# Two more weight slots during the first attention of a fused two-block transformer kernel

## The chip, the cores and the metric

The kernel runs as one program on one core of a Trainium2 chip. The metric is the device time of one execution in microseconds (us); the median of three runs of the kernel before is 869.89 us, the lowest 868.91 and the highest 870.24. The profile that is read below is one execution of its own: it took 870.59 us, of which 868.7 us lie between its first and its last instruction (the span).

## The reference, cut to what matters

256 tokens of width 1024 in float32 go through two blocks. The first block is where the change lies:

```python
h = layer_norm(x, ln0_g, ln0_b)
proj = h @ w_in + b_in                    # split into qa, ka, va, qb, kb, vb, ga, gb
y_na  = neighbourhood_attention(qa, ka, va, rpb) @ w_branch_na
y_swa = windowed_gqa_with_sink(rope(qb), rope(kb), vb, sink) @ w_branch_swa
mixed = sigmoid(ga) * y_na + sigmoid(gb) * y_swa
h = layer_norm(ALPHA * h + mixed @ w_out + b_out, ln1_g, ln1_b)
h = layer_norm(ALPHA * h + relu(h @ w_ff1 + b)**2 @ w_ff2 + b, ln2_g, ln2_b)
```

The second block (a pooling mixer, a second attention, two convolutional feed-forward layers) follows and is computed by the same weight machinery.

## The kernel before, in words

All matrix products are kept near float32 accuracy by splitting both operands into a high part of type fp32r and a low part, the rest (`whi`, `wlo` for weights; `xh`, `xl` and the like for data), and by three matmuls per product: high by high, high by low, low by high (`mm3`, L367).

Weights come as a list of chunks of 128 x 1024 float32 (512 KB), numbered in the order in which the program uses them. The class `Weights` (L76) moves each chunk through three places. A raw buffer takes the DMA from memory (six such buffers for the first 48 chunks, then four); the load of chunk i + 6 is issued on the SP queue behind the split of chunk i. Splitting a chunk takes one instruction on ScalarE, the copy to `whi` (L133), and then one on VectorE, the subtraction that gives `wlo` (L143). The results lie in a slot (8 KB per partition) until the matmuls that use the chunk are done and `free` gives the slot back. There are seven slots, w0 to w6, in the pool `pers`; after the first attention two more and an extra one are added in the pool `late`, which takes over memory of the first attention.

The order of all instructions of every engine is the order of the Python program, and every engine runs its instructions in that order. So the splits have to be written somewhere, and this is done by `pump(most, eng, keep)`: it splits the next chunks, at most `most`, while more than `keep` slots are free. `unit_a` (L374) is the unit of work: it computes 256 output columns in two halves (m = 0 and 1) of 128. A half issues its matmuls into one PSUM bank, then calls the epilogue that empties the bank, then pumps: at most two chunks and keeping two slots (`KEEP`), or one in the units `bna`. With `ahead` the copy to `whi` is issued before the epilogue and the subtraction behind the epilogue's first part. The matmuls of a half go to one of four banks that are used in rotation (`bank`, tag "a").

The first attention uses chunks 0 to 41: qa and ka (0 to 7), va (8 to 11), qb and kb/vb (12 to 17), the gates ga (18 to 25), the branch `bna` (26 to 29: four units of one chunk, so eight halves of 12 matmuls each), the gates gb (30 to 37), and the last branch `swa` (38 to 41, again eight halves of 12 matmuls). The product with `w_out` uses chunks 42 to 49 (matmuls of 512 columns, `Acc`, L446).

A loop of ten steps (L752) carries the softmax work of eight head pairs: at step i the transposes of pair i - 2, the scores of pair i, the normalisation of pair i - 1, then units as fillers, then the product with the values of pair i - 2 (`pv1`). The fillers of step 6 are the four units of `bna`. Its epilogue (L644) is one VectorE instruction per half that reads the bank. The four `swa` units come after the loop; their epilogue (L784 to L791) is, per half, two VectorE instructions, one copy on ScalarE (`mixh`) and a third VectorE instruction (`mixl`).

The pools `att1o` and `att1` hold the first attention's data; both close behind `swa` (L799). In `att1` lie, among others, `row` (the first norm's gain, used once at the start), `va` (the values of the first four head pairs, last read by `pv1` of pair 3 in step 5), `mix` (two buffers) and ten buffers `fm`.

Of the kernel before, what the change touches and what calls it, by code (L numbers as in the profile page):

```python
# [5 lines left out]
F32 = mybir.dt.float32  # L6
# [6 lines left out]
P = 128  # L13
T = 256
D = 1024
# [3 lines left out]
LENT_FOR = 48  # L19
NW = 7  # L20
NW_LATE = 2
KEEP = 2
TAIL = 6
TAIL_FF = 8
# [51 lines left out]
class Weights:  # L76


    def __init__(self, nc, pool, wts, lent):
        self.lent, self.done = lent, 0  # L80
        self.nc, self.pool, self.wts, self.n = nc, pool, wts, wts.shape[0]
        self.raw, self.ready, self.slots, self.held = {}, {}, [], []
        self.loaded = self.split = self.taken = self.n_slots = 0
        self.before, self.gain, self.retired, self.todo, self.eager = {}, {}, set(), [], True
        self.at_split = set()
# [26 lines left out]
            self.before[i](self.raw[i])  # L112

    def pump(self, most=99, eng=None, keep=0):
        while most and len(self.slots) > keep and self.split < self.n:
            most -= 1
            self.high()(eng)

    def high(self):

        i = self.split
        while i in self.todo:
            self.prepare(1)
        r = self.raw.pop(i)
        slot = self.slots.pop(0)
        pool, tag = slot
        hi = pool.tile([P, 1024], F32R, tag=tag + "h", name="whi", bufs=1)
        lo = pool.tile([P, 1024], F32R, tag=tag + "l", name="wlo", bufs=1)
        for j, g in enumerate(self.gain.get(i, [])):
            d = slice(j * T, (j + 1) * T)  # L130
            self.nc.scalar.activation(out=hi[:, d], in_=r[:, d], func=AF.Identity, scale=g)
        if i not in self.gain:
            self.nc.scalar.activation(out=hi, in_=r, func=AF.Copy)  # L133
        self.ready[i] = (hi, lo, slot)
        self.split += 1

        def low(eng=None):
            for j, g in enumerate(self.gain.get(i, [])):
                d = slice(j * T, (j + 1) * T)
                self.nc.vector.scalar_tensor_tensor(out=lo[:, d], in0=r[:, d], scalar=g, in1=hi[:, d].bitcast(F32),  # L140
                                                    op0=ALU.mult, op1=ALU.subtract)
            if i not in self.gain:
                (eng or self.nc.vector).tensor_tensor(out=lo, in0=r, in1=hi.bitcast(F32), op=ALU.subtract)  # L143
            self.done += 1
            self.load()
        return low

    def highs(self, n):
        return [self.high() for _ in range(min(n, len(self.slots), self.n - self.split))]

    def take(self, k, c):

# [27 lines left out]
def model(tc, x_in, wts, bvec, cols_in, const_in, nab_in, pos_in, out):  # L180
    nc = tc.nc
    from contextlib import ExitStack
    with ExitStack() as top:
# [6 lines left out]
        def rot(pool, shape, dt, tag, name, bufs):  # L190

            key = (id(pool), tag)
            i = turn[key] = (turn.get(key, -1) + 1) % bufs
            return pool.tile(shape, dt, tag=f"{tag}_{i}", name=name, bufs=1)
# [4 lines left out]
        def pad(pool, n):  # L199

            pool.tile([P, 8 * n], F32, name=f"pad_{len(pads)}", tag=f"pad_{len(pads)}", bufs=1)
            pads.append(n)
# [6 lines left out]
        ctx_g, ctx_x = ExitStack(), ExitStack()  # L209
        gpool = ctx_g.enter_context(tc.tile_pool(name="gates", bufs=1))  # L210
        opool = ctx_x.enter_context(tc.tile_pool(name="att1o", bufs=1))
        apool = ctx_x.enter_context(tc.tile_pool(name="att1", bufs=1))

        pad(com, PAD_COM)
# [2 lines left out]
        def scratch():  # L217
            return rot(com, [P, D], F32, "scr", "scr", 4)

        def vec(row, eng=None, pool=None, tag="bv", bufs=4):  # L220
            v = rot((pool or com), [P, D], F32, tag, f"v{row}", bufs)
            (eng or nc.gpsimd).dma_start(out=v, in_=bvec[row:row + 1, :].broadcast_to([P, D]))
            return v

        for t in range(2):
            x_t.append(scratch())
        for s in HALF:
            nc.sync.dma_start(out=x_t[0][:, s], in_=x_in[0:P, s])
        row = apool.tile([1, D], F32, name="row")
        nc.scalar.dma_start(out=row, in_=bvec[V_G0:V_G0 + 1, :])  # L230
        b0 = vec(V_B0, nc.sync)
        W = Weights(nc, pers, wts, [(com, "scr_2"), (com, "scr_3")])
        W.grow(pers, NW)
        W.load(3)
        nc.sync.dma_start(out=x_t[1], in_=x_in[P:T, :])
        W.load(NRAW + 2 - 3)
# [137 lines left out]
        def unit_a(kx, epi, nk=8, pump=(2, None), ahead=0):  # L374

            cs = [W.take(4, 256) for _ in range(nk // 4)]
            for m in range(2):
# [9 lines left out]
                for low in lows:  # L387
                    low()
                W.pump(0 if ahead else pump[0], pump[1], keep=KEEP)
                for f in later:  # L390
# [55 lines left out]
        class Acc:  # L446
# [15 lines left out]
            def both(self, k, x):  # L462
# [3 lines left out]
                W.free(c)  # L466
                W.pump(2, keep=KEEP)

# [27 lines left out]
        lows = W.highs(2)  # L496
# [19 lines left out]
        def load_const(pool, name, at, n, shape=None):  # L516
            c = pool.tile([P, n], F32, name=name)
            nc.sync.dma_start(out=c, in_=const_in[:, at:at + n])
            const[name] = c
            return c  # L520
# [3 lines left out]
        def load_nab(p):  # L524
            nab[p] = rot(apool, [P, 2, 384], F32, "nab", "nab", 2)
            nc.sync.dma_start(out=nab[p], in_=nab_in[p])
# [4 lines left out]
        fm = {}  # L531
# [34 lines left out]
        nc.sync.dma_start(out=vab, in_=bvec[V_VAB:V_VAB + 1, 0:512].broadcast_to([P, 512]))  # L566


        va = apool.tile([P, 2, 512], F32, name="va")
        vb = apool.tile([P, 2, P], F32, name="vb")  # L570

        def f_va():
# [143 lines left out]
        def transp1(p):  # L716
            pt = soft[p][0]
            ptT[p] = []
            for e in range(2):
                b = bank("b")  # L720
                for s in range(2):
                    for j in range(2):
                        nc.tensor.transpose(out=b[:, s * T + j * P:s * T + (j + 1) * P],
                                            in_=pt[e][:, j, s * P:(s + 1) * P], identity=ident)
                c = rot(apool, [P, 512], F32, "pT", "pT", 2)
                nc.scalar.activation(out=c, in_=b, func=AF.Copy)
                ptT[p].append(c)
# [13 lines left out]
        def step(n=1):  # L741
            for _ in range(n):
                next(fill, None)
# [8 lines left out]
        for i in range(10):  # L752
            if i == 1:
                swam = load_const(apool, "swam", K_SWA, 512)
                sink = few.tile([P, 24], F32, name="sink")
                nc.sync.dma_start(out=sink, in_=bvec[V_SINK:V_SINK + 1, 0:24].broadcast_to([P, 24]))
                bout = vec(V_BOUT, nc.sync)
            if i == 6:
                g1 = vec(V_G1, nc.sync)
                b1 = vec(V_B1, nc.sync)  # L760
            if i >= 2:
                transp1(i - 2)
            if i < 8:
                scores1(i)
                if i + 2 < 4:
                    load_nab(i + 2)
            if 1 <= i <= 8:
                normalise(i - 1, lambda a, j: a[:, j, :], apool)
            if i in (3, 5):
                t = i // 2 - 1  # L770
                nc.vector.scalar_tensor_tensor(out=x_t[t], in0=x_t[t], scalar=ALPHA, in1=bout, op0=ALU.mult,
                                               op1=ALU.add)
            step(plan[i][0] + plan[i][1])
            if i >= 2:
                pv1(i - 2)
# [4 lines left out]
        def swa_epi(u):  # L780
            def epi(m, o):
                i = 2 * u + m
                g, z = gate["gb", i], gate["ga", i]
                nc.vector.scalar_tensor_tensor(out=g, in0=g, scalar=1.0, in1=o[:, :T], op0=ALU.add, op1=ALU.mult)  # L784
                s = rot(apool, [P, T], F32, "mix", "mix", 2)
                nc.vector.tensor_tensor(out=s, in0=g, in1=z, op=ALU.add)
                hi = rot(gpool, [P, T], F32R, "ga", "mixh", 8)
                lo = rot(gpool, [P, T], F32R, "gb", "mixl", 8)
                nc.scalar.activation(out=hi, in_=s, func=AF.Copy, scale=0.5)
                mixed[i] = (hi, lo)  # L790
                return [lambda: nc.vector.scalar_tensor_tensor(out=lo, in0=s, scalar=0.5, in1=hi.bitcast(F32),  # L791
                                                               op0=ALU.mult, op1=ALU.subtract)]
            return epi
# [2 lines left out]
            unit_a(lambda k: att[4 + k], swa_epi(u), 4, ahead=1)  # L796


        ctx_x.close()  # L799
        late = top.enter_context(tc.tile_pool(name="late", bufs=1, side="right"))  # L800
        pad(late, 14)
        X = [late.tile([P, D], F32, name=f"X{t}") for t in range(2)]
        W.grow(late, NW_LATE)
        ctx_w = ExitStack()
# [266 lines left out]
        lows = W.highs(2)  # L1071
# [265 lines left out]
        lows = []  # L1337
        for i in range(10):
# [15 lines left out]
            lows = W.highs(2)  # L1354
# [197 lines left out]
```

## Time and profile before

| what | us |
|---|---|
| median of three runs | 869.89 |
| the profiled execution | 870.59 |
| its span, first to last instruction | 868.7 |
| TensorE busy in the span | 834.3 |
| VectorE busy | 637.0 |
| ScalarE busy | 490.2 |

Stretches of the span that matter here: the loads and first norm to 38 us, the loop of ten steps from 44 to 155 us, `bna` from 113.7 to 124.9 us, `swa` from 155.4 to 168.1 us, the product with `w_out` from 168.1 to about 192 us. "PE" is TensorE, "DVE" VectorE, "ACT" ScalarE; a row of the timeline merges equal neighbours, with their count.

### The profile page before, as it was taken

What the parts mean: (1) busy time and instruction counts of PE and PEld (TensorE: products, weight loads), DVE (VectorE), ACT (ScalarE), POOL (GpSimd) and SP (SyncE); (2) the same over time, 40 slices, a digit from 0 to 9 for tenths busy, and PEclk for the clock granted to TensorE, in tenths of its full rate; (3) what the DMA queues carried; (4) which work ended last, traced back from release to release, by engine and by line L of the source; (5) the groups of instructions that cost most, each with busy time, mean ns of one, the idle gap of its engine ahead of it and who ended that gap; (6) DMA issues with size and microseconds to landing.
All of it is one profiled execution on the core that took longest, in us unless ns stands there. A gap on an engine that the chain in (4) does not pass through costs nothing.

```text
span 868.7 us, 15167 instructions
## 1 busy us (share of the span) xinstructions
PE 834.3 (96%) x5872; PEld 755.4 (87%) x5872; DVE 637.0 (73%) x1118; ACT 490.2 (56%) x905; POOL 73.8 (8%) x97
## 2 busy tenths in 40 slices
PE   5999999999999999989999999999999999999997
PEld 3889889879889999878999999988776999999995
DVE  5575884786828888886899777664896689977772
ACT  4465666444625447455676655555785566765551
POOL 0003000002000000010000000138620000000000
PEclk9999999999999999999999999999999999999999
DMA  7583462557616666623557565434252456756531
GB/s 284 191 314 138 135 205 99 170 172 298 218 53 227 208 219 219 215 98 128 179 185 261 173 216 184 156 124 132 80 208 81 167 176 212 242 197 216 180 113 48
DMA packets 43896, 154.60 MB, mean 178 GB/s; under 512 B 5009, under 2 KB 5905, under 8 KB 43826
## 3 DMA queue, kind: packets, MB, share of 16 engines
q1 hardware_dynamic: 41616, 146.90, 49.6%
q0 software_dynamic: 1632, 5.93, 2.0%
q8 instruction: 46, 0.75, 0.4%
q10 hardware_dynamic: 578, 0.82, 0.3%
q14 instruction: 24, 0.20, 0.1%
HBM read 152.58 MB, written 1.05 MB: 177 GB/s over the span
## 4 chain that ended last, share of the span: by engine, by line
PE 41%; DVE 7%; ACT 6%; issue 2%; DMA 1%; POOL 0%; DVEq 0%; POOLq 0%; ACTq 0%
PE bank_a L372 22%; PE bank_b L372 15%; DVE wlo L143 3%; PE bank_a L427 2%; ACT whi L133 2%; DMA wraw<-wts_dram 1%; ACT p L1304 1%; ACT scr L305 1%; DVE p L1292 1%; DVE p L712 1%; PE bank_a L351 1%; DVE cv L1117 1%; PE bank_a L1325 0%; DVE cv L1115 0%; DVE X L334 0%
## 5 line engine op out<-in xcount | busy, mean ns | idle before, releaser
L143 DVE TENSOR_TENSOR wlo<-wraw,whi 128x1024 fp32r<-128x1024 f32 x261 | 312.3, 1226 | 82.7 <-ACT whi L133 82.1
L372 PE MATMUL bank_a<-xh,whi 128*128 128x256 f32 x1056 | 296.4, 281 | 1.8 <-DVE cv L1117 1.6
L372 PE MATMUL bank_a<-xh,wlo 128*128 128x256 f32 x1056 | 293.4, 278 | 0.6 <-DVE wlo L143 0.5
L372 PE MATMUL bank_a<-xl,whi 128*128 128x256 f32 x1056 | 293.3, 278 | 0.0
L133 ACT ACTIVATE whi<-wraw 128x1024 fp32r<-128x1024 f32 x261 | 264.5, 1049 | 25.0 <-DMA wraw<-wts_dram 22.2
L372 PEld LDWEIGHTS bank_a<-xh,whi 128*128 128x128 f32 x1056 | 198.8, 188 | 7.3 <-ACT whi L133 2.6
L372 PEld LDWEIGHTS bank_a<-xl,whi 128*128 128x128 f32 x1056 | 198.6, 188 | 1.7
L372 PEld LDWEIGHTS bank_a<-xh,wlo 128*128 128x128 f32 x1056 | 198.6, 188 | 1.0 <-DVE wlo L143 1.0
L1114 ACT ACTIVATE cv<-bank_a,cols 128x256 f32<-128x256 f32 x76 | 42.0, 559 | 81.4 <-PE bank_a L372 81.2
L372 PE MATMUL bank_b<-wlo,ah 128*128 128x512 f32 x176 | 69.4, 395 | 0.0
L372 PE MATMUL bank_b<-whi,al 128*128 128x512 f32 x176 | 69.1, 393 | 0.0
L372 PE MATMUL bank_b<-whi,ah 128*128 128x512 f32 x176 | 68.7, 390 | 0.0
L1115 DVE SCALAR_TENSOR_TENSOR cv<-bank_a,cols,cv 128x255 f32<-128x255 f32 x76 | 36.5, 480 | 43.3 <-ACT cv L1114 43.1
L372 PE MATMUL bank_b<-whi,uh 128*128 128x512 f32 x128 | 50.0, 390 | 1.4 <-ACT uh L341 1.4
L372 PE MATMUL bank_b<-wlo,uh 128*128 128x512 f32 x128 | 50.5, 394 | 0.0
L372 PE MATMUL bank_b<-whi,ul 128*128 128x512 f32 x128 | 50.4, 393 | 0.0
L269 POOL TENSOR_TENSOR rstd<-ve,neghalf 128x1 f32<-128x1 f32 x22 | 13.4, 611 | 391.2 <-DVE ve L310 248.6
L341 ACT ACTIVATE uh<-ur 128x256 fp32r<-128x256 f32 x32 | 13.2, 412 | 59.1 <-DVE ur L911 44.3
L890 POOL TENSOR_SCALAR wraw<-wraw,cols 128x256 f32<-128x256 f32 x28 | 30.2, 1096 | 165.5 <-DVE cv L1115 160.0
L372 PEld LDWEIGHTS bank_b<-wlo,ah 128*128 128x128 f32 x176 | 33.2, 188 | 6.7
L1117 DVE SCALAR_TENSOR_TENSOR cv<-bank_a,cols,cv 128x254 f32<-128x254 f32 x76 | 36.6, 482 | 2.7
L372 PEld LDWEIGHTS bank_b<-whi,al 128*128 128x128 f32 x176 | 33.1, 188 | 6.3
(199 smaller groups left out, 1253.4 us busy)
## 6 DMA issues: line engine op xcount, KB each, us to landing
wraw<-wts_dram SPq DMA_DIRECT2D x268, 512.0 KB, 4.5
v<-bvec_dram POOLq DMA_DIRECT2D x10, 512.0 KB, 5.3
v<-bvec_dram SPq DMA_DIRECT2D x4, 512.0 KB, 6.9
nab<-nab_dram SPq DMA_DIRECT2D x4, 384.0 KB, 5.6
poolA<-const_dram POOLq DMA_DIRECT2D x1, 544.0 KB, 8.4
scr<-x_dram SPq DMA_DIRECT2D x2, 256.0 KB, 3.1
scr<-x_dram SPq DMA_DIRECT2D x1, 512.0 KB, 9.8
out_dram<-X SPq DMA_DIRECT2D x2, 256.0 KB, 2.1
```

What stands on the lines that cost most here:

```text
L133: self.nc.scalar.activation(out=hi, in_=r, func=AF.Copy)
L143: (eng or self.nc.vector).tensor_tensor(out=lo, in0=r, in1=hi.bitcast(F32), op=ALU.subtract)
L269: nc.gpsimd.tensor_tensor(out=r, in0=v, in1=neghalf, op=ALU.pow)
L305: nc.scalar.activation(out=junk[:, HALF[q if into is None else into]], in_=src, func=AF.Square, scale=1.0 / 32.0, accum_out=ss[:, q:q + 1])
L341: nc.scalar.activation(out=hi, in_=src, func=AF.Copy)
L351: nc.tensor.transpose(out=b[:, j * P:(j + 1) * P], in_=h[:, k * P:(k + 1) * P], identity=ident)
L372: nc.tensor.matmul(o, lhsT=l, rhs=r, start=start and i == 0, stop=stop and i == 2)
L427: nc.tensor.matmul(o[:, :256], lhsT=self.kx(k)[b][:, t * P:(t + 1) * P], rhs=self.cs[u][k // 4][a][:, k % 4, :], start=i == 0 and k == 0, ...
L890: nc.gpsimd.tensor_scalar(out=d, in0=d, scalar1=g, scalar2=None, op0=ALU.mult)
L1114: nc.scalar.activation(out=v, in_=o[:, :T], func=AF.Identity, scale=col(c + 2), bias=col(c + 3))
L1115: nc.vector.scalar_tensor_tensor(out=v[:, 1:T], in0=o[:, 0:T - 1], scalar=col(c + 1), in1=v[:, 1:T], op0=ALU.mult, op1=ALU.add)
L1117: nc.vector.scalar_tensor_tensor(out=v[:, 2:T], in0=o[:, 0:T - 2], scalar=col(c), in1=v[:, 2:T], op0=ALU.mult, op1=ALU.add)
```

## The change

The kernel gets two more slots that exist only while the first attention's memory does. Slot w7 lies in a new pool `att1w` between `att1o` and `att1` and is there from the start. Slot w8 lies in `att1`, on two buffers of 4 KB (`wide`) that until then hold `row` and `va`; it is lent at step 6 of the loop. A slot that is lent may take chunks up to 41 only (`LAST_SWA`): `usable` leaves it out for later ones, and `pump`, `high` and `highs` go by `usable` instead of by the list of free slots. The product of gate and branch in `swa` (`mix`) moves from two buffers of its own to the ten `fm` buffers.

```diff
+LAST_SWA = 41
     def pump(self, most=99, eng=None, keep=0):
-        while most and len(self.slots) > keep and self.split < self.n:
+        while most and len(self.usable()) > keep and self.split < self.n:
...
-        slot = self.slots.pop(0)
+        slot = self.usable()[0]
+        self.slots.remove(slot)
...
     def highs(self, n):
-        return [self.high() for _ in range(min(n, len(self.slots), self.n - self.split))]
+        lows = []
+        while len(lows) < n and self.usable() and self.split < self.n:
+            lows.append(self.high())
+        return lows
+
+    def usable(self):
+        return [s for s in self.slots if self.split <= self.until.get(s[1], self.n)]
+
+    def lend(self, pool, last):
+        self.grow(pool, 1)
+        self.until[self.slots[-1][1]] = last
...
+        wpool = ctx_x.enter_context(tc.tile_pool(name="att1w", bufs=1))
...
+        wide = [apool.tile([P, D], F32, tag=f"w{NW + 1}" + p, name="wide", bufs=1) for p in "hl"]
...
-        row = apool.tile([1, D], F32, name="row")
+        row = wide[0][0:1, :]
...
         W.grow(pers, NW)
+        pad(wpool, 2)
+        W.lend(wpool, LAST_SWA)
...
-        va = apool.tile([P, 2, 512], F32, name="va")
+        va = wide[1].rearrange("p (t c) -> p t c", t=2)
...
             if i == 6:
+                W.lend(apool, LAST_SWA)
...
-                s = rot(apool, [P, T], F32, "mix", "mix", 2)
+                s = rot(apool, [P, T], F32, "fm", "mix", 10)
...
+        assert W.taken == LAST_SWA + 1
         ctx_x.close()
```

## Rows read from the trace of the kernel before

**Rows 1.** The page: the span, and the busy time of TensorE.
```profile
span 868.7 us, 15167 instructions
...
PE 834.3 (96%) x5872; PEld 755.4 (87%) x5872; DVE 637.0 (73%) x1118; ACT 490.2 (56%) x905; POOL 73.8 (8%) x97
```

**Rows 2.** Waits of TensorE, 0 to 200 us: total, times, longest.
```profile
PE bank_a L351 <- DVE scr L287: 8.1, 1, 8.1
...
PE bank_a L372 <- DVE gb L784: 0.9, 2, 0.6
```

**Rows 3.** Timeline around the unit ka23: start, length, work, [idle before <- releaser].
```profile
43.95 0.47 ACT L536 ACTIVATE fm_ka<-bank_a,cols 128x256 f32<-128x256 f32 x1 [2.25 <-PE bank_a L372]
...
45.40 2.36 DVE L143 TENSOR_TENSOR wlo<-wraw,whi 128x1024 fp32r<-128x1024 f32 x2 [2.83 <-ACT whi L133]
```

**Rows 4.** Timeline of TensorE in bna: halves 4, 5 and 6, and pv1.
```profile
119.33 0.28 PE L372 MATMUL bank_a<-oh,whi 128*128 128x256 f32 x1
...
120.69 0.28 PE L372 MATMUL bank_a<-oh,whi 128*128 128x256 f32 x1
...
122.05 0.28 PE L372 MATMUL bank_a<-oh,whi 128*128 128x256 f32 x1
...
124.86 1.08 PE L734 MATMUL bank_a<-pT,vb 128*64 128x256 f32 x8
```

**Rows 5.** Timeline of VectorE in bna.
```profile
118.03 0.74 DVE L644 SCALAR_TENSOR_TENSOR ga<-ga,bank_a 128x256 f32<-128x256 f32 x2
120.12 1.23 DVE L143 TENSOR_TENSOR wlo<-wraw,whi 128x1024 fp32r<-128x1024 f32 x1 [1.36 <-ACT whi L133]
121.27 0.75 DVE L644 SCALAR_TENSOR_TENSOR ga<-ga,bank_a 128x256 f32<-128x256 f32 x2
121.93 1.22 DVE L143 TENSOR_TENSOR wlo<-wraw,whi 128x1024 fp32r<-128x1024 f32 x1
123.06 0.75 DVE L644 SCALAR_TENSOR_TENSOR ga<-ga,bank_a 128x256 f32<-128x256 f32 x2
```

**Rows 6.** Timeline of ScalarE in bna: four copies to whi.
```profile
119.05 3.89 ACT L133 ACTIVATE whi<-wraw 128x1024 fp32r<-128x1024 f32 x4
```

**Rows 7.** Timeline of TensorE in swa and the product with w_out.
```profile
155.40 0.28 PE L372 MATMUL bank_a<-oh,whi 128*128 128x256 f32 x1
...
163.76 0.28 PE L372 MATMUL bank_a<-oh,wlo 128*128 128x256 f32 x1
164.42 0.36 PE L372 MATMUL bank_a<-oh,whi 128*128 128x256 f32 x1 [0.38 <-DVE gb L784]
...
166.59 0.39 PE L372 MATMUL bank_a<-oh,whi 128*128 128x256 f32 x1 [0.55 <-DVE gb L784]
...
176.76 0.40 PE L372 MATMUL bank_b<-wlo,mixh 128*128 128x512 f32 x1
177.58 0.51 PE L372 MATMUL bank_b<-whi,mixh 128*128 128x512 f32 x1 [0.42 <-ACT whi L133]
...
178.84 0.50 PE L372 MATMUL bank_b<-wlo,mixh 128*128 128x512 f32 x1 [0.53 <-DVE wlo L143]
```

**Rows 8.** Timeline of VectorE in swa.
```profile
163.86 0.42 DVE L784 SCALAR_TENSOR_TENSOR gb<-gb,bank_a 128x256 f32<-128x256 f32 x1
...
170.53 0.42 DVE L786 TENSOR_TENSOR mix<-gb,ga 128x256 f32<-128x256 f32 x1
170.87 1.22 DVE L143 TENSOR_TENSOR wlo<-wraw,whi 128x1024 fp32r<-128x1024 f32 x1
172.01 0.42 DVE L791 SCALAR_TENSOR_TENSOR mixl<-mix,mixh 128x256 fp32r<-128x256 f32 x1
...
175.97 0.42 DVE L791 SCALAR_TENSOR_TENSOR mixl<-mix,mixh 128x256 fp32r<-128x256 f32 x1
```

**Rows 9.** Timeline of ScalarE in swa.
```profile
170.99 0.42 ACT L789 ACTIVATE mixh<-mix 128x256 fp32r<-128x256 f32 x1 [0.34 <-DVE mix L786]
...
176.47 2.96 ACT L133 ACTIVATE whi<-wraw 128x1024 fp32r<-128x1024 f32 x3 [1.10 <-DVE mixl L791]
```

**Rows 10.** All exponentials on the buffers p: length min/median/max in ns.
```profile
L696 ACT ACTIVATE p<-p,mx x32: 492/496/512, 49.2 to 131.7; 128x256 f32<-128x256 f32 x32
```

More of the change, by code (lines that the diff above doesn't have):

```diff
@@ L81, in __init__ @@
         self.nc, self.pool, self.wts, self.n = nc, pool, wts, wts.shape[0]
-        self.raw, self.ready, self.slots, self.held = {}, {}, [], []
+        self.raw, self.ready, self.slots, self.held, self.until = {}, {}, [], [], {}
         self.loaded = self.split = self.taken = self.n_slots = 0
```

## The prediction

> **What bounds the kernel now.** I read the page first: TensorE is busy for 834.3 us of the 868.7 us span [rows 1], so a change is worth what it adds to or takes from the 34 us in which TensorE waits, and work on other engines counts only where TensorE waits for it. Next the waits of TensorE over the first 200 us [rows 2]: the long one, 8.1 us, is the first norm at the start, which the change doesn't touch. Between 38 and 155 us the same view has no wait at all, so there is nothing to win in the loop of ten steps; there the change can only cost. The first later waits are two for the `swa` epilogue, 0.9 us together. Then the timeline of TensorE [rows 7]: after those two it stops twice more, at 177.58 us for the copy to `whi` of chunk 49 and at 178.84 us for its subtraction. Last the timelines of VectorE and ScalarE beside these places [rows 5, 6, 8, 9], because each runs in program order and what stands ahead of a late instruction is what makes it late.
>
> **What moves.** I counted free slots through the program, before and after. With slot w7 the condition "more than two free" is met one half earlier, at the first half of unit ka23: one more split there, and from then on every split is the same instruction place with the next chunk. With slot w8 it is met again at the first half of `bna`: halves 0 and 1 now split one chunk each, where before only half 1 did; halves 3, 5 and 7 split one as before. The two are paid back when chunk 42 comes up, for which lent slots don't count: the second half of gb2 splits one chunk instead of two, and half 5 of `swa` splits none instead of one. The last half of gb3 splits two, and halves 0, 1, 2, 3 and 7 of `swa` one each, before and after. At the end of `swa` 49 chunks are split in both. Nothing is added in total: two splits (1.05 us on ScalarE, 1.22 us on VectorE each) move earlier, and two loads on the SP queue with them.
>
> **The split at ka23.** It comes behind the first half's epilogue. ScalarE then sits idle for 2.25 us and VectorE for 2.83 us [rows 3]; both hold it. Cost 0. Without that cover the softmax of pair 0 would be 1.2 us later, and TensorE takes it only two steps on. The load that goes one place ahead of the bias and rope tables on SP delays these by one chunk; they are used in step 1 and later, over 10 us on. The split dropped in gb2 frees VectorE where it is idle anyway: 0.
>
> **The split at half 0 of bna.** VectorE comes late out of the softmax: its epilogues of halves 0 and 1 start together at 118.03 us, one 0.33 behind the other, though TensorE was done with both banks before [rows 5]. Four banks rotate, so half 5 of TensorE needs the epilogue of half 1, and at 120.69 us [rows 4] it has it (118.36 + 0.42 = 118.78 us): 1.9 us of lead. Now a subtraction stands between the two epilogues. It needs its copy, and ScalarE's first copy runs from 119.05 us to about 120.1 [rows 6], so the subtraction starts at 120.12 us, as the one behind half 1 does now, and the next VectorE instruction follows at 121.27. The epilogue of half 1 ends at 121.69 us. In `swa` TensorE started 0.14 us after such an epilogue (163.86 + 0.42 to 164.42), and its first matmul after the wait took 0.36 us instead of 0.28 [rows 7, 8]. So half 5 starts at 121.83 us, 1.14 late, and 0.08 goes at the restart. Half 6 would then start at 123.27. Its bank is emptied by the epilogue of half 2, behind the second subtraction: 121.60 + 1.14 = 122.74, ended 123.16, seen by TensorE at 123.30: 0.03 more. From there VectorE needs 1.8 us for two halves and TensorE 2.7, so the lag closes, and `pv1` (half 4's bank, free at about 125.0) comes at 126.1 instead of 124.86 [rows 4]. Sum +1.25 us, with no later wait to take it up before 164 us. Bounds: 0 if the lead were enough after all, 2.9 (121.27 - 118.36) if none of it counted. I take 1.25, the value with the lead that the rows show.
>
> The Trainium skill says that independent groups of matmuls should rotate through PSUM banks so that the emptying of one overlaps the next group's matmuls (Perfetto Trace Analysis, Matmuls). By that rule this epilogue stays hidden and the sum is the gain below alone. The two waits for L784 show four banks in rotation failing to cover a late epilogue, so I go by the rows.
>
> **The split dropped in swa.** The two waits at 164.42 and 166.59 us come from VectorE's work up to the epilogue of half 3, which is the same before and after: they stay, 1.26 us (0.54 and 0.72 between the end of the pace of 0.12 us and the restart). At half 5 the subtraction at 170.87 us goes. The `mixl` behind it can't start at once: its `mixh` runs on ScalarE from 170.99 to 171.41 us [rows 9], because the mix ends at 170.95 [rows 8]. So `mixl` comes at 171.45 instead of 172.01: 0.56 us, not 1.22. Everything of halves 6 and 7 follows at once on VectorE, and the last `mixl` moves from 175.97 to 175.41. ScalarE's copy for chunk 49 waits 1.10 us for just that `mixl` [rows 9], since its slot lies in memory that the first attention gives back as a whole; `fm` buffers hold the mix afterwards, in the same pool, so that wait stays and the copy moves from 176.47 to 175.91, done 176.96. TensorE arrives at 176.76 + 0.23 = 176.99: the wait for the copy goes, what is late next is the subtraction, also 0.56 earlier, and TensorE resumes at 178.28 instead of 178.84. Gain 0.56 us. Bounds: 0 if another wait ends last there, 1.4 if both waits went (178.84 - 176.99 - two matmuls of 0.23). Behind it VectorE's norm waits for TensorE, and the loads for VectorE's subtractions, so I let the whole rest move along.
>
> **Addresses.** The buffers of `att1` move by some 4 to 8 KB. The 32 exponentials on four buffers at different places took 492 to 512 ns [rows 10]; at 20 ns on each of 32 this is 0.6 us on ScalarE, either way, under its idle time. I take 0. The wider rotation of `mix` removes no wait that the rows show: 0.
>
> **Sum.** +1.25 - 0.56 = +0.69 us. The profiled execution of 870.59 us (span 868.7) would become 871.3 (span 869.4). It lies 0.70 above the median 869.89, so the median is forecast at 870.6 us. About 0.2% (1.7 us) is what a measurement of this kernel can tell from no change.
>
> **Rivals.**
> - Evacuation covered: ScalarE or VectorE reach half 0 of `bna` earlier than I read, and half 5 has its bank. For it: TensorE now has 1.9 us of lead; against it: the lead is smaller than the 2.9 us by which the epilogue moves. Then only the gain stands: 869.3 us.
> - Slots were what was short. All four stops from 164 to 179 us go: 1.26 + 0.59 + 0.80 (two of `swa`, then 177.58 - 176.99, then the rest of the 1.4) = 2.6 us, so 867.3 us with no cost in `bna`. For it: TensorE stops for `whi` and `wlo` there. Against it: chunk 49 may not use a lent slot, and the first two stops are for the epilogue. The Trainium skill's rule that a repeated bubble on the saturated engine can mean too few buffers (Perfetto Trace Analysis, Optimization Strategy) would speak for this; the trace does not agree, as the releaser in `swa` is L784 in both waits.
> - Slower: the new stop in `bna` changes TensorE's pace. Two paces stand in the trace: 12 matmuls in 1.36 us in `bna`, 113.3 ns each [rows 4], and from 155.40 to 163.76 us 71 steps in 8.36 us, 117.7 ns [rows 7]. If the restart at half 5 brought the slow one, it would hold through 36 matmuls of `bna`, 144 of gb0 to gb2 and the last 24 of `swa`: 204 x 4.4 ns = 0.9 us on top, 871.5 us. With more than about 240 such matmuls it passes 0.2%. Against it: the trace goes on at the fast pace after the stops at 164 and 166 us.
> - The change does not do what it says: splits wait for data, so that places change but times don't: 869.9 us. Against it: in `bna` the copies run one behind the other without a gap for a load [rows 6].
>
> **How the numbers follow.** Forecast (870.6) 0.52; cost without gain, 871.1, 0.06; evacuation covered 0.17; slots short 0.06; slow pace 0.12; no effect 0.07. Within 0.2% lie all but the slots-short case and the upper half of the slow pace, with tails from the spread of the runs (868.91 to 870.24): faster by over 0.2% 0.08, within 0.2% 0.76, slower 0.16. The range goes from 868.9 (below the covered case, by half the spread) to 872.0 (above the slow pace by the same): it leaves out the slots-short case and the ends of the tails.
>
> **What would show it.** In the trace after: one L644 ahead of the first subtraction in `bna` and a wait of TensorE for L644 of about 1 us at half 5, with `pv1` some 1.2 us later; the two waits for L784 in `swa` as before; no subtraction in halves 4 to 6 of `swa`; no stop for the copy of chunk 49 and a stop of about 0.8 us for its subtraction. No wait at L644 makes the first step wrong; a time below 868.5 would mean that the stops in `swa` were for slots, one above 872 a stop that I haven't seen.

## The result, and the profile after

The change took 875.3 us (874.22 to 876.15, 4 runs) against 870.07 us of the kernel before in the same comparison: ratio 1.0053, 95% interval 1.0032 to 1.0074. The forecast was 870.6 us, a change of less than 0.2%, and its range ended at 872.0. Two later comparisons of the same two kernels gave 1.0019 (0.9996 to 1.0042) and 1.0038 (1.0021 to 1.0055): slower, but by less than the first one said.

The page of after, beside [rows 1]: TensorE is busy 4.7 us longer with the same 5872 matmuls, and the span grew by 5.0. What was lost is hardly waiting: TensorE's idle time is 34.4 us of the span before and 34.7 after.

```profile
span 873.7 us, 15164 instructions
...
PE 839.0 (96%) x5872; PEld 759.1 (87%) x5872; DVE 637.2 (73%) x1118; ACT 490.2 (56%) x905; POOL 73.5 (8%) x97
```

The waits of TensorE over the first 200 us, after (line 644 of before is now 663, 784 is 804, 372 is 391, 143 is 145):

```profile
PE bank_a L391 <- DVE gb L804: 1.2, 2, 0.6
...
PE bank_a L391 <- DVE ga L663: 0.7, 1, 0.7
PE bank_b L391 <- DVE wlo L145: 0.5, 1, 0.5
```

Beside [rows 2], the two waits for the `swa` epilogue are still there, and the one for L663 is new, as forecast. VectorE in `bna`, after, beside [rows 5]: the subtraction stands between the epilogues of halves 0 and 1.

```profile
118.66 0.41 DVE L663 SCALAR_TENSOR_TENSOR ga<-ga,bank_a 128x256 f32<-128x256 f32 x1
120.77 1.23 DVE L145 TENSOR_TENSOR wlo<-wraw,whi 128x1024 fp32r<-128x1024 f32 x1 [1.69 <-ACT whi L135]
121.91 0.42 DVE L663 SCALAR_TENSOR_TENSOR ga<-ga,bank_a 128x256 f32<-128x256 f32 x1
122.24 1.22 DVE L145 TENSOR_TENSOR wlo<-wraw,whi 128x1024 fp32r<-128x1024 f32 x1
123.37 0.75 DVE L663 SCALAR_TENSOR_TENSOR ga<-ga,bank_a 128x256 f32<-128x256 f32 x2
```

TensorE, after: half 5 of `bna`, which ran on without a stop in [rows 4], and the three stops from the first wait for L804 to chunk 49, where [rows 7] have four. The stop for the copy of chunk 49 is gone, the one for its subtraction stays.

```profile
121.41 0.28 PE L391 MATMUL bank_a<-oh,wlo 128*128 128x256 f32 x1
122.38 0.39 PE L391 MATMUL bank_a<-oh,whi 128*128 128x256 f32 x1 [0.69 <-DVE ga L663]
...
166.70 0.39 PE L391 MATMUL bank_a<-oh,whi 128*128 128x256 f32 x1 [0.60 <-DVE gb L804]
...
168.96 0.39 PE L391 MATMUL bank_a<-oh,whi 128*128 128x256 f32 x1 [0.58 <-DVE gb L804]
...
180.87 0.51 PE L391 MATMUL bank_b<-wlo,mixh 128*128 128x512 f32 x1 [0.52 <-DVE wlo L145]
```

VectorE in `swa`, after, beside [rows 8]: the mix of half 4, then half 5, behind which there is no subtraction any more, so that `mixl` waits for `mixh`, and the last `mixl`.

```profile
170.76 0.41 DVE L804 SCALAR_TENSOR_TENSOR gb<-gb,bank_a 128x256 f32<-128x256 f32 x1
171.20 0.42 DVE L806 TENSOR_TENSOR mix<-gb,ga 128x256 f32<-128x256 f32 x1
...
172.46 0.41 DVE L804 SCALAR_TENSOR_TENSOR gb<-gb,bank_a 128x256 f32<-128x256 f32 x1
172.97 0.43 DVE L806 TENSOR_TENSOR mix<-gb,ga 128x256 f32<-128x256 f32 x1
173.88 0.42 DVE L811 SCALAR_TENSOR_TENSOR mixl<-mix,mixh 128x256 fp32r<-128x256 f32 x1 [0.48 <-ACT mixh L809]
...
177.99 0.42 DVE L811 SCALAR_TENSOR_TENSOR mixl<-mix,mixh 128x256 fp32r<-128x256 f32 x1
```

All programs of this study run the same 5872 matmuls in the same order, so a stage can be measured as the time between the starts of the same two matmuls in each trace. With the repeats told below there are 3 traces of the kernel before and 5 of the change. The stage limits are times in the trace of [rows 1 to 9], the first of before and the one that the forecast was made on; all numbers are in us:

| stage | before, 3 traces | change, 5 traces | means differ by |
|---|---|---|---|
| 0 to 57.6 | 57.61 to 58.51 | 57.08 to 58.45 | -0.04 |
| 57.6 to 87.4 | 29.82 | 29.82 to 29.83 | 0.01 |
| 87.4 to 113.7 (ga1 to ga3) | 26.25 | 26.86 | **+0.61** |
| 113.7 to 128.0 (`bna`) | 14.29 to 14.63 | 15.56 to 15.65 | **+1.09** |
| 128.0 to 149.6 (gb0 to gb2) | 21.67 to 21.88 | 22.06 to 22.25 | **+0.43** |
| 149.6 to 166.6 (gb3, `swa`) | 16.94 | 16.74 to 16.95 | -0.12 |
| 166.6 to 178.8 (`swa`, w_out) | 12.25 to 12.26 | 11.90 to 11.91 | **-0.35** |
| 178.8 to 211.1 | 32.21 to 32.53 | 32.21 to 32.53 | 0.15 |
| 211.1 to 346.1 | 133.45 to 135.04 | 133.37 to 134.06 | -0.27 |
| 346.1 to 412.1 | 66.02 to 66.04 | 66.18 to 67.91 | **+0.83** |
| 412.1 to 441.1 | 28.87 to 29.17 | 29.37 to 29.45 | **+0.42** |
| 441.1 to 587.3 (conv layer 0) | 145.97 to 146.18 | 145.98 to 149.05 | +1.10 |
| 587.3 to 722.1 | 133.92 to 134.84 | 133.56 to 135.21 | 0.07 |
| 722.1 to the end (conv layer 1) | 146.33 to 149.42 | 146.31 to 146.74 | -1.01 |
| span | 868.82 (mean) | 871.74 (mean) | +2.92 |

In the bold rows the two kernels' traces don't overlap. With three traces against five, a row that is pure chance does that in 2 of 56 orders, so one such row among 14 would be no surprise. The experiments bear out the first four bold rows as the program's; the two behind 346 us are taken up at the end. The rows of conv layers 0 and 1 are luck, as is told below. In the first pair of traces, which has the one that the forecast was made on, that luck fell the wrong way: 2.9 us are conv layer 0 (149.05 against 146.18), and 1.0 came back between 211 and 346 us (134.06 against 135.04).

### The profile page after: what moved, and what is told of

It is laid out like the page before. It is cut to its first block, busy times and chain, and to the rows that moved or that the text cites. A ratio compares the mean times of both kernels' runs of the same rounds, so it can differ in the third digit from the quotient of the medians.

```text
span 873.7 us, 15164 instructions
## 1 busy us (share of the span) xinstructions
PE 839.0 (96%) x5872; PEld 759.1 (87%) x5872; DVE 637.2 (73%) x1118; ACT 490.2 (56%) x905; POOL 73.5 (8%) x97
## 4 chain that ended last, share of the span: by engine, by line
PE 40%; DVE 9%; ACT 5%; issue 2%; DMA 2%; POOL 0%; DVEq 0%; POOLq 0%; ACTq 0%
PE bank_a L391 22%; PE bank_b L391 14%; DVE wlo L145 3%; PE bank_a L446 2%; DMA wraw<-wts_dram 2%; ACT whi L135 1%; ACT scr L324 1%; DVE p L1313 1%; ACT p L1325 1%; DVE p L731 1%; PE bank_a L370 1%; DVE cv L1138 1%; DVE cv L1136 0%; DVE X L353 0%; POOL rstd L288 0%
## 5 line engine op out<-in xcount | busy, mean ns | idle before, releaser
L391 PEld LDWEIGHTS bank_b<-whi,ah 128*128 128x128 f32 x176 | 33.0, 188 | 6.1
```

What stands on the lines that cost most here:

```text
L391: nc.tensor.matmul(o, lhsT=l, rhs=r, start=start and i == 0, stop=stop and i == 2)
```

## The experiments

**First: is the loss the program's, and which part's?** The trace of after showed the pace of TensorE, not its waits. A run of 256-column matmuls goes at one of two paces at a granted clock of 1.00: 113.3 ns from start to start (each then lasts 276 or 277 ns in the trace) or 117.7 ns (281 ns). The theories were ADDRESS (the moved buffers set the pace), ORDER (the places of the splits set it), and as rival STOP (the new stop in `bna` is the loss). First the change again, unaltered:

> The changed kernel once more, unaltered. Its first profile against the profile of the kernel before: TensorE is busy 4.7 us longer, almost the whole difference of the spans (5.0), because units of 256-column matmuls run at one of two paces, about 113.3 or 117.7 ns a matmul at a granted clock of 1.00, and other units got the slow one. If the pace of a unit is fixed by the program: 875 +- 1, the same units slow (ga1 to ga3, gb0 to gb2, conv layer 0 from 441 to 559). If it is chance from one execution to the next: another set of slow units, with a time that moves by several us between the runs.

Measured: 873.72 us (870.34 to 877.48, 10 runs), 1.0019 (0.9996 to 1.0042). Neither answer holds whole: from 57.6 to 211 us the trace takes 155.69 us where the first took 155.76, and conv layer 0 does not repeat (145.99 us where the first took 149.05). Then the layout alone:

```diff
+        wpool = ctx_x.enter_context(tc.tile_pool(name="att1w", bufs=1))
...
-        pad(wpool, 2)
-        W.lend(wpool, LAST_SWA)
+        pad(wpool, 258)
...
-                W.lend(apool, LAST_SWA)
```

> The first attention's memory lies where the change puts it, the products of the second attention's epilogue rotate through the buffers that the change uses, but no slot is lent, so every split stands where it stood before. Theory ADDRESS (the moved buffers set the slow pace): TensorE busy about 839, 874 to 875. Theory ORDER (the places of the splits set it): busy about 834, 869 to 870.5, with ga1 to ga3 and conv layer 0 as in the kernel before. Rival STOP (the new stop in the second branch pass and the waits around it are the loss): also 869 to 870.5, since that stop is not there.

Measured: 871.79 us, 0.9993 (0.9973 to 1.0012). ga1 to ga3 took 26.86 us, exactly as in the change, with no slot lent; `bna` 14.28, without a stop; gb0 to gb2 22.06. So ADDRESS holds in its stage, but not for the whole time: it had given 874 to 875. The counterpart, slots and order without the move:

```diff
-        wpool = ctx_x.enter_context(tc.tile_pool(name="att1w", bufs=1))
         apool = ctx_x.enter_context(tc.tile_pool(name="att1", bufs=1))
+        wpool = ctx_x.enter_context(tc.tile_pool(name="att1w", bufs=1))
...
-        wide = [apool.tile([P, D], F32, tag=f"w{NW + 1}" + p, name="wide", bufs=1) for p in "hl"]
...
-        row = wide[0][0:1, :]
+        row = apool.tile([P, D], F32, tag=f"w{NW + 1}h", name="row", bufs=1)[0:1, :]
...
-        va = wide[1].rearrange("p (t c) -> p t c", t=2)
+        va = apool.tile([P, D], F32, tag=f"w{NW + 1}l", name="va", bufs=1).rearrange("p (t c) -> p t c", t=2)
```

> Both slots lent as in the change, with its order of splits, but the first attention's tiles lie at their addresses of before (the slot that goes ahead of them is behind them). Theory ADDRESS: TensorE busy about 834, only the stop of 0.7 in the branch pass stays and the gain of 0.35 at the end of the second attention: 870 to 871. Theory ORDER: the slow units stay, 874 to 876. Rival STOP: 874 to 876, since the stop stays.

Measured: 872.02 us, 1.0002 (0.998 to 1.0024). ga1 to ga3 took 26.25, as before; the stop in `bna` is there (15.57); the gain behind it too (16.76 and 11.91). ORDER is turned down for ga1 to ga3: the layout alone has the old order and the slow pace, the slots in place have the new order and the fast one. And the second slot lent one step later, so that `bna` has its old splits:

```diff
-            if i == 6:
+            if i == 7:
                 W.lend(apool, LAST_SWA)
+            if i == 6:
                 g1 = vec(V_G1, nc.sync)
```

> As the change, but the second slot is lent one step later, so that the extra split falls into the first half after the branch pass and not between two of its epilogues. Rival STOP: the wait of 0.7 at half 5 of the branch pass goes and with it most of the loss, 870 to 871. Theory ORDER: the split's new place may change the pace of any unit, 871 to 876, and the pass before the split (ga1 to ga3) stays as slow as in the change. Theory ADDRESS: the wait goes, worth 0.7 to 1.2, the slow units stay: 874 to 874.6.

Measured: 871.74 us, 0.9996 (0.9976 to 1.0015). Its waits from 80 to 200 us show no stop for the `ga` epilogue and one for `gb` instead of two:

```profile
PE bank_a L391 <- DVE gb L805: 0.6, 1, 0.6
PE bank_b L391 <- DVE wlo L145: 0.5, 1, 0.5
```

`bna` took 14.63 us, so the stop is worth 0.9 to 1.0 us (1.3 against the 14.28 of the layout alone, whose `bna` ran at the fast pace); ga1 to ga3 stayed at 26.86, and gb0 to gb2 at 22.25 with no restart ahead of them. ADDRESS had given 874 to 874.6 us here, too much again. By time the three variants can't be told apart from the kernel before, which took 871.63 us in this comparison: their ratios lie within 0.1% of 1, with intervals of 0.2% to either side. The stages decide.

**Second: do these hold in repeats?**

> The kernel before once more, unaltered, for a second trace of it. Theory ADDRESS (the first attention's place sets the pace of its branch passes): ga1 to ga3 at the fast pace again, 26.25 us from the start of ga1 to that of bna, as the two programs with the old addresses have had it, where the four with the new ones all took 26.86. Theory CHANCE (each execution draws its paces): 26.25 or 26.86, evens. The wait of 1.4 us before ff1's unit at 218: there again if the program sets it, which would make the change 1.2 better than its stages from 57 to 194 say; gone if that trace had bad luck. The ratio to the other runs of the same kernel is 1.000, and what it misses that by is the error of such a comparison.

Measured: 870.41 us against 870.6 us of its own kernel, 1.0000 (0.9982 to 1.0018), which says how far such a comparison is to be trusted. ga1 to ga3 took 26.25 us again. The wait of 1.4 us at 218 us is not in this trace. Conv layer 1, fast in the first trace, was slow in this one, for 3 us.

> The changed kernel a third time, with more runs. From 57 to 194 us it took 2.0 more than before in both traces: 1.1 for the stop in the second branch pass, 1.3 for slow units, 0.4 won at the end of the second attention. If those are the program's and the rest is drawn: 138.9 again in that stretch, against 136.9; the ratio to before 1.001 to 1.0025, not 1.005; conv layer 0 in 118 or 121 by chance.

Measured: 873.64 us (871.78 to 878.05), 1.0038 (1.0021 to 1.0055). From 57 to 194 us it took 138.9 us, as expected; the ratio lies above what was expected.

Old addresses and the later slot together (the two diffs above):

> Both edits that took something from the loss, together: the first attention's tiles at their old addresses, and the second slot lent one step later. Theories ADDRESS and STOP: ga1 to ga3 fast (26.25), no stop in the second branch pass (14.3 rather than 15.6), the end of the second attention 0.9 shorter than before, so some 0.8 below the kernel before over 57 to 194 us: ratio 0.998 to 1.000. Theory CHANCE: no stop, pace as it falls, ratio 0.997 to 1.003.

Measured: 871.27 us, 1.0010 (0.9994 to 1.0026). The stages are as expected (26.25; 14.63; 28.3 from 149.6 to 178.8 against 29.2), 0.4 us below the mean of the kernel before from 57.6 to 211; the time is not below, and misses the ratio that was expected. It doesn't beat the kernel before.

The layout with `pad(wpool, 130)` for `pad(wpool, 258)`:

> As the layout alone, with the first attention's tiles moved by half as much (4160 bytes rather than 8256). Theory ADDRESS, any shift: ga1 to ga3 slow, 26.86. Theory ADDRESS, this shift alone: fast, 26.25. No stop in the second branch pass in either. Ratio 0.999 to 1.002.

Measured: 873.54 us, 1.0033 (1.0015 to 1.0051), which misses the ratio; in its trace conv layer 1 is slow (149.43 against 146.3). ga1 to ga3 took 26.86: the half move does the same.

**Third: what of the move?** 8256 and 4160 bytes have 64 bytes over a multiple of 4096 in common. `pad(wpool, 256)`:

> As the layout alone, no slot lent, but the first attention's tiles moved by 8192 bytes, where 8256 and 4160 bytes (both 64 more than a multiple of 4096) gave the slow pace in ga1 to ga3. Theory ALIGNMENT (the 64 bytes do it): fast, 26.25 us from the start of ga1 to that of bna, about 153.7 from 57.6 to 211, ratio 1.000 to 1.001. Theory PLACE (any other place does it): slow, 26.86, about 155.0, ratio 1.001 to 1.003.

`pad(wpool, 2)`:

> As the layout alone, no slot lent, with the first attention's tiles moved by 64 bytes. ALIGNMENT: slow, 26.86, about 155.0 from 57.6 to 211, ratio 1.001 to 1.003. PLACE: slow too, or fast (26.25) if so small a move is none. Fast here with slow for 8192 bytes would turn ALIGNMENT down.

Measured: 871.04 us, 1.0010 (0.9996 to 1.0023), and 870.81 us, 1.0016 (1.0001 to 1.0030). The matmuls of ga1 to ga3, from 90 us on (count: shortest/median/longest in ns): first one form of them in the kernel before and in the change, then two forms for the move by 8192 bytes, then two for the one by 64:

```profile
L372 PE MATMUL bank_a<-xh,wlo x42: 275/277/279, 89.8 to 110.4; 128*128 128x256 f32 x42
...
L391 PE MATMUL bank_a<-xh,wlo x42: 280/281/282, 89.9 to 111.0; 128*128 128x256 f32 x42
```

```profile
L390 PE MATMUL bank_a<-xl,whi x45: 276/276/280, 89.9 to 111.5; 128*128 128x256 f32 x45
L390 PE MATMUL bank_a<-xh,wlo x45: 276/276/279, 90.0 to 111.6; 128*128 128x256 f32 x45
```

```profile
L390 PE MATMUL bank_a<-xl,whi x44: 277/281/281, 89.9 to 111.7; 128*128 128x256 f32 x44
L390 PE MATMUL bank_a<-xh,wlo x44: 281/281/282, 90.0 to 111.8; 128*128 128x256 f32 x44
```

The stage takes 26.25 us against 26.86: the 64 bytes set its pace, not the 8 KB. In all four layouts `wide` also holds `row` and `va` ahead of the rest, so that the tiles which lay between those two before move 4096 bytes further than the others. The clean pair is therefore 8192 against 8256 bytes, which differ by 64 bytes in every tile of `att1` and in nothing else; it gives the same 26.25 and 26.86. In `bna` this pair goes the other way (14.63 and 14.28), which takes part of the loss back: from 57.6 to 211 it is 154.2 us for 8192 bytes and 154.95 to 154.97 for 64, 4160 and 8256 bytes. By time the two can't be told apart.

So the change without its pad:

```diff
-        pad(wpool, 2)
         W.lend(wpool, LAST_SWA)
```

> The change without its pad of 64 bytes: the same slots, splits and stop, with the first attention's tiles 8192 bytes from their old place. ALIGNMENT: ga1 to ga3 fast, the stop of 1.06 and the gain of 0.35 as they were, about 154.6 from 57.6 to 211 instead of 155.7, ratio to before 1.001 to 1.002. PLACE: 155.7 and 1.002 to 1.004, as the change.

Measured: 872.54 us, 1.0031 (1.0018 to 1.0045), a ratio that PLACE had given. The execution that was traced took 1186.22 us at a mean granted clock of 0.66, so that its stages can't be set beside the others; a second trace of the same kernel:

> The change without its pad of 64 bytes, a second trace. ALIGNMENT: ga1 to ga3 in 26.25, about 154.6 from 57.6 to 211. If a split in ga1 breaks the fast pace, as it did in part where the second slot came later (26.66): 26.7 and 155.2.

Measured: 872.55 us, 155.44 us from 57.6 to 211, hardly better than the change (155.45 to 155.77). ga1 runs at the fast pace to its end; inside ga2 the pace turns slow, with no wait of TensorE there, so that ga1 to ga3 take 26.66. The stage ahead, 57.6 to 87.4, takes 30.05 us where the kernel before and the change took 29.82 or 29.83. Two rows, one from ga1 and one from ga2 and ga3:

```profile
L390 PE MATMUL bank_a<-xh,wlo x15: 276/276/276, 89.4 to 94.2; 128*128 128x256 f32 x15
...
L390 PE MATMUL bank_a<-xh,wlo x25: 279/281/283, 99.9 to 111.8; 128*128 128x256 f32 x25
```

Without the pad the first lent slot itself lies 64 bytes lower; that this turns ga2 was not tried. With the second slot lent later as well:

> The change without the pad and with the second slot lent one step later. ALIGNMENT and STOP: 153.4 from 57.6 to 211, 0.3 below before, ratio 0.999 to 1.001. PLACE: 154.2 or more, as the slot lent later with the pad (154.4), ratio 1.000 to 1.002.

Measured: 871.19 us, 1.0022 (1.0009 to 1.0035), a ratio above that of either theory (its trace has conv layer 0 at the slow pace), and 153.9 us from 57.6 to 211, between the two. ga2 turns at the same matmul (26.66 again, and 30.05 ahead of it). Dropping the pad is no remedy.

**Fourth: what lies behind 211 us?** Two more traces of the change and one of the kernel before:

> The change, a fourth trace. Theory DRAWN (the pace behind 211 us falls anew in each execution): 155.7 from 57.6 to 211 as always, conv layer 0 from 441 in 118.0 or 120.8, conv layer 1 from 722 in 138.1 or 141.0, either way. Rival PROGRAM (the change makes them slow more often): slow in one of them at least.

> The change, a fifth trace: the same two theories and numbers as for the fourth. Under DRAWN the two need not agree with each other.

> The kernel before, a third trace. DRAWN: 153.4 to 154.0 from 57.6 to 211 again, conv layers 0 and 1 fast or slow, as its second trace had layer 1 slow (141.0) and its first had not. The wait of 1.4 us before ff1's unit at 218 not there, as in all traces but the first.

Measured: 874.35 and 875.77 us for the change, 869.97 for the kernel before. The change took 145.98 and 149.05 us for conv layer 0 (441 to 587) and 146.3 and 146.5 for conv layer 1 to the end; the kernel before took 146.18 and 146.33, and 154.10 from 57.6 to 211, without the 1.4 us wait. The same program, in three traces (first, second and fifth of the change, conv layer 0, 462 to 555 us):

```profile
L391 PE MATMUL bank_a<-xh,wlo x178: 280/281/282, 461.8 to 554.8; 128*128 128x256 f32 x178
```

```profile
L391 PE MATMUL bank_a<-xh,wlo x180: 276/276/281, 461.9 to 553.3; 128*128 128x256 f32 x180
```

```profile
L391 PE MATMUL bank_a<-xh,wlo x178: 281/281/282, 461.8 to 554.8; 128*128 128x256 f32 x178
```

And the kernel before, second trace, conv layer 1 (726 to 794 us), where its first had 275/277/284:

```profile
L372 PE MATMUL bank_a<-xh,wlo x130: 281/281/282, 725.9 to 793.6; 128*128 128x256 f32 x130
```

Of the 17 traces that can be compared, 6 have one such stage at the slow pace (conv layer 0 three times, conv layer 1 twice, 258 to 346 us once), 1.7 to 3.1 us each, in kernels of every kind. DRAWN holds for them: one program has conv layer 0 at either pace. The rival PROGRAM asked for a slow one in at least one of the two, and that came true as well. Whether the lent slots make conv layer 0 slow more often (3 of 10 traces with a slot lent, 0 of 7 without) so few traces don't tell.

The rows from 346 to 441 us are another matter, since all traces of before lie below those of the change there. From 346 to 412 the difference goes with TensorE's granted clock. Four stretches of it in the third trace of before and then in the third of the change. The columns are the stretch, its length, the busy time (x instructions) of PE, PEld, DVE, ACT and POOL, the granted clock, the share of the DMA engines and GB/s:

```profile
382.00:384.00 2.00, 1.26 (x9) 1.17 (x9) 0.56 (x2) 1.65 (x6) 0.44 (x1) 0.85 0.00 0
384.00:386.40 2.40, 2.40 (x13) 2.40 (x13) 2.21 (x4) 2.27 (x3) 0.55 (x1) 0.50 0.00 0
386.40:388.00 1.60, 0.86 (x6) 0.67 (x4) 1.60 (x3) 1.21 (x4) 0.00 (x0) 0.86 0.54 69
388.00:390.00 2.00, 1.92 (x16) 1.92 (x17) 1.23 (x4) 1.61 (x4) 0.55 (x1) 1.00 0.51 207
```

```profile
385.40:387.80 2.40, 1.37 (x13) 1.23 (x12) 2.22 (x4) 2.24 (x3) 0.55 (x1) 1.00 0.00 0
387.80:389.40 1.60, 0.28 (x1) 0.08 (x1) 1.60 (x3) 1.23 (x4) 0.00 (x0) 1.00 0.59 115
389.40:391.40 2.00, 1.95 (x9) 1.95 (x10) 1.24 (x3) 1.58 (x4) 0.55 (x1) 0.50 0.42 170
391.40:393.40 2.00, 2.00 (x14) 2.00 (x13) 2.00 (x3) 0.00 (x0) 0.00 (x0) 0.65 0.00 0
```

In both, TensorE waits for VectorE here. In before the clock falls to its lower level (0.50, 1.2 GHz) after the first, short wait, and 13 slow matmuls fill time in which TensorE would have waited anyway. In the change it falls only after the second, long wait, and the slow matmuls come in the open: 66.71 against 66.03 us for the stage (the price is read from this pair; no run moves the clock alone). The second, third and fifth trace of the change have it so (66.71 to 66.75); in the fourth the clock is at 0.50 in both places (67.91), in the first it is covered (66.18). All three traces of before have it covered, and the layout with 8256 bytes too (66.02); the eight other traces took 66.40 to 66.79. The clock is not all of it: with 0.50 in both places the layouts moved by 64 and by 8192 bytes took 66.40 us, the slot lent later 66.70. The last piece, 0.42 us at 430 us, is a longer stall of TensorE for the convolution's sum on VectorE. In the change VectorE pauses ahead of that sum. Here are one row of before and one of the change:

```profile
428.65 0.43 DVE L1122 TENSOR_TENSOR cv<-cv 128x256 f32<-128x256 f32 x1
```

```profile
431.11 0.43 DVE L1143 TENSOR_TENSOR cv<-cv 128x256 f32<-128x256 f32 x1 [0.46 <-DVE cv L1138]
```

The releaser that the row names is VectorE itself, so what it waited for is not shown. TensorE idles 1.3 us for that sum in all five traces of the change, 0.7 to 1.0 in those of before, and 1.0 to 1.7 in the other variants. The pause is in the traces of all variants, of those without a lent slot and of those at the old addresses too, and in none of before. So neither the slots nor the move brings it. Among what all variants share with the change is the mix on the `fm` buffers, which was not tried alone; why there is a pause stays open.

## Why the prediction was wrong, point by point

- **What bounds the kernel: right, and too narrow.** "A change is worth what it adds to or takes from the 34 us in which TensorE waits" left out the 834 us in which it works. The two paces stood in the rows and were used for a rival only. A time above 872 was to mean "a stop that I haven't seen"; it was no stop, as TensorE's idle time grew by 0.3 us.
- **The split at ka23, cost 0: right.** 57.6 to 87.4 us takes 29.82 and 29.83.
- **The split at half 0 of `bna`, +1.25: right in mechanism, 1.09 in size** (1.36 against the trace that the forecast was made on). The order on VectorE is the forecast one. The epilogue of half 1 ends at 122.33 and TensorE restarts 0.05 later, not 0.14. The mean is smaller since two of the three traces of before run `bna` at the slow pace (14.63 us against 14.29), where TensorE arrives later by itself. The lend one step later takes the stop away: shown. The Trainium skill's rule that a rotation through banks lets the emptying overlap the next matmuls (Perfetto Trace Analysis, Matmuls) would have had no stop; the trace has one of 0.69 us beside the slow restart.
- **The split dropped in `swa`, -0.56: right in mechanism, -0.35 in size** (-0.47 with the stage ahead of it, whose traces overlap). Both L804 waits stay. In halves 5 to 7 the mix starts 0.51 us after the start of its epilogue (172.46 to 172.97) instead of 0.44 as in half 4 (170.76 to 171.20): three times 0.07.
- **The failing step: "Addresses ... I take 0."** I looked at the exponentials of ScalarE and not at what TensorE reads. The scores' matmuls right ahead of ga1 read `fm` buffers that moved; what ga1 to ga3 themselves read in the layouts, `xT` and the seven old slots, did not move. Nor was the move 4 to 8 KB: it is 8256 bytes, and 12352 for the tiles between `row` and `va`. Where I had 0, 64 bytes alone make ga1 to ga3 0.61 us longer: shown by the layouts moved by 8192 and 8256 bytes. gb0 to gb2 are some 0.3 longer in the moved layouts (22.06 against 21.67 to 21.88). The rival "the new stop in `bna` changes TensorE's pace" had the size (0.9) and the wrong cause: gb0 to gb2 are as slow without the stop.
- **"I let the whole rest move along": wrong.** From 346 to 441 us the change's traces show 0.83 and 0.42 us more, with the clock and the stall above. Why is open. I took the whole rest to follow TensorE's arrival; that the clock falls elsewhere because of a later arrival is not shown, and the layouts without a slot lent have the pause of VectorE too.
- **The size of the result.** 0.69 was forecast; the stages from 57.6 to 211 say 1.8, those to 441 us 2.8, and the mean of the traces 2.9, in line with 1.0019 and 1.0038. The spans of the first pair differ by 5.0: against the 0.69 forecast, conv layer 0 brought 2.9 by bad luck, and ga1 to ga3 and gb0 to gb2 1.2 by the pace. The 1.0053 of the first comparison has luck in it too: all four of its runs took 874.2 us or more, and of 21 later runs of the change 10 did. Only one of the four has a trace, so what the other three lost stays open. The forecast's spread (868.91 to 870.24) came from three runs; 31 later ones went from 869.8 to 876.77. The range was to end half that spread (0.67) outside two of the rivals, which gives 868.6 to 872.2 and not 868.9 to 872.0; the result lies above either.

## What to carry to other kernels

Where TensorE is busy for 96% of the span, a change of layout may be a change of its pace, and the matmuls' durations tell: compare the median duration of the same matmuls, stage by stage, ahead of any wait. Measure stages between the same matmuls in several traces of both kernels; where the ranges don't overlap the program is the likely cause, to be borne out by a variant; elsewhere it may be the draw, and a single pair of traces can't tell the two apart. The extra piece of work on VectorE between two epilogues was paid at the next use of the bank, as the lead worked out from the rows had said.

## What was not expected of the hardware

- 256-column matmuls run at 113.3 or 117.7 ns at the same granted clock of 1.00. A pace can hold for long, over 90 us and some 530 matmuls in conv layer 0, and it can turn with no wait in between, as inside ga2 of the change without its pad.
- In ga1 to ga3, 64 bytes in the place of the first attention's buffers decide it, and the same way in every trace: 26.86 us for moves by 64, 4160 and 8256 bytes (9 traces of 5 programs), 26.25 for none and 8192 (6 traces of 4 programs); only the two traces with slots lent at the move by 8192 lie between (26.66). Why 64 bytes do it is open.
- In the conv layers the pace differs from execution to execution of one program, at 3 us a layer (145.98 or 149.05 us).
- A drop of the granted clock to 0.50 came without loss where it fell into a stretch in which TensorE would wait for VectorE (66.03 us), and with a stage 0.7 us longer where it came after that stretch (66.71).
